# Loads in pieces between the weight tiles, squares of two chunks at a time, and low parts ahead of the next addition in a Trainium2 kernel of stacked transformer blocks

## The chip, the core and the metric

The kernel runs on one core of one Trainium2 chip. The core has five engines that each work through their own list of instructions in order: TensorE (PE, matrix products), VectorE (DVE), ScalarE (ACT), GpSimd (POOL) and SyncE (SP, which here only issues DMAs). An instruction waits on semaphores for results of other engines, and whatever stands behind it on its engine waits too. The metric is the device time of one execution in microseconds (us), lower is better. TensorE's clock is granted in two levels, 2.4 and 1.2 GHz; the profile shows it as 1.00 and 0.50.

## The reference

256 tokens (B = 1, S = 256) of width 2048 pass through two stacks of two layers each. Memory is a second sequence of 256 rows. The weights are float32 and together some 540 MB, so that each is read once.

```python
def first_block(x, mem, ...):
    memn = rms_norm(mem, norm_memory)
    for i in range(DEPTH):                       # DEPTH = 2
        h = rms_norm(x, norm_mix[i])
        if i % 2 == 0: x = x + pool_mixer(h, pool_w[ia], pool_scale[ia])
        else:          x = x + dsa_attention(h, attn_w_in[ib], attn_w_out[ib], ...)
        x = x + memory_cross_attention(rms_norm(x, norm_xattn[i]), memn, ...)
        x = x + swiglu(rms_norm(x, norm_ffn[i]), ffn_w_in[i], ffn_w_out[i])
    return rms_norm(x, norm_final)

def rms_norm(x, g):
    y = xf * lax.rsqrt(jnp.mean(xf * xf, axis=-1, keepdims=True) + EPS)
    return (y * g).astype(x.dtype)
```

The second stack follows on the result: per layer a norm, one wide input projection, four attention mixers (dilated, stick-breaking, MoBA, forgetting), and an output projection that is added back.

## The kernel before

**Layout.** The residual stream lies transposed in `XT`, 16 chunks of 128 channels by 256 tokens. Every product is computed in three parts for accuracy: an operand is split into a high part (fp32r, written by ACT, `split` L388) and a low part, the rest (written by DVE, L389). An operand chunk is thus 128x512, `[hi|lo]`; for weights ACT makes `whi` (L184) and DVE `wlo` (L194) from the raw tile `wraw`. TensorE multiplies `whi` with `[hi|lo]` and `wlo` with `hi`.

**Weights.** `Net.plan` lists all weight tiles (mostly 128x1024 float32, 512 KB) in the order of use. `_dma_to`, `_split_to` and `_lo_to` (L169 to L194) load, copy and subtract the next ones; `ahead` says how far each runs in front of the tile in use. All loads are issued by SP, in the order of the program. Raw tiles have 4 buffers.

**Start.** `mem_prep` loads the memory transposed (`memT`, 4 pieces of 512 KB) in turn with the first 4 weight tiles, then `cst`, the memory by rows (`memn`, 2 MB), the tokens by rows (`xn`, 2 MB), `band`, and then weight tiles in turn with pieces of `xT`. `kv_v` (L331, L336) computes the memory's values over 4 weight groups `xv`; beside it `mem_norm` squares `memn` on ACT (L599), and DVE computes the factor `Mn` (L587 to L416), which L430 spreads over the partitions. Four units of keys (`kv_k`) follow.

**Pool mixer.** `pool_gen` squares `xn`, computes the factor `xr`, scales `band` with it (L670, DVE), multiplies `xn` with `band` on TensorE (L677, L679) and splits the results into `X`; `pool_mix` multiplies them with the pool weights (L303 to L306) and adds into `XT` (L696).

**Residual additions.** After an output projection, `resid_pair` adds two chunks at a time from PSUM into `XT` (L506, 128x512), where the next stage's operands are split by `prep`: ACT's high parts at once, DVE's low parts later, from the list `late` that `flush` empties. `flush(1)` at the next product leaves one low part waiting. `sq_acc` squares the chunks for the next norm, the even ones on POOL (L400), the odd ones on ACT (L398), and POOL adds each to `acc` (L402, 128x256). `rowsum` (L422) sums `acc` over the partitions with two products; DVE then takes the inverse root. This happens at the stages called pool, x0 (cross attention, layer 0), x1 and b0 (second stack, layer 0); after the FFNs and the DSA attention `resid` does it with single chunks (L500, L501). With the next norm `fin` (the final norm of the first stack and the first of the second together) there are two sums, `acc` and `acc2`.

**Second stack.** Before it, at L1368 to L1381, SP loads the head gains `hg`, `fbias`, constants, `blk` and `masks`; DVE scales `hg` (L1370) and ACT copies the masks to `stickr` and `diagr`.

## Time and profile before

| what | value |
|---|---|
| time, median of 3 runs (lowest to highest) | 3086.33 us (3086.14 to 3092.42) |
| the profiled execution: time, span | 3085.38 us, 3083.5 us |
| PE busy | 3035.1 us, 98% of the span |
| DVE, ACT, POOL busy | 66%, 51%, 22% |
| mean granted clock of TensorE | 0.995 |
| read from HBM | 537.66 MB, 175 GB/s over the span |

The span is what the profiler sees from the first to the last instruction; the time of the execution is 1.9 us longer, and the median of the runs 0.95 us longer again. TensorE is busy nearly all the time, so what can be won beside fewer columns lies in two things: the few stretches in which it waits, and the few in which its clock is at 0.50, where the same column takes twice as long. Both are found by going along PE's timeline with its idle times, and along the granted clock.

### The profile page before, as it was taken

How to read it: one execution, taken by the hardware profiler on the slowest of the kernel's cores; microseconds unless marked ns; L12 is line 12 of the kernel's file. 1: busy time of each engine (PE TensorE's matmuls, PEld its weight loads, DVE VectorE, ACT ScalarE, POOL GpSimd, SP SyncE). 2: the span in 40 equal slices, each digit the busy share in tenths (PEclk: the TensorE clock that was granted, in tenths of full speed). 3: DMA queues.
4: the chain of work that ended last, by engine and by line, in shares of the span. 5: the costliest groups of instructions: out<-in, count | busy, mean ns of one | idle time of the engine just before them, and what ended most of it. 6: DMA issues, size and time to landing. Idle time of an engine off the chain costs nothing. (4 is left out here: it accounts for less than half of the span.)

```text
span 3083.5 us, 46498 instructions
## 1 busy us (share of the span) xinstructions
PE 3035.1 (98%) x17546; PEld 2646.8 (86%) x17546; DVE 2040.1 (66%) x3043; ACT 1558.1 (51%) x2470; POOL 687.5 (22%) x647
## 2 busy tenths in 40 slices
PE   7999999999999999999999999999999999999999
PEld 6888888888888888888888888888878888887888
DVE  5867555555567978755555555766786676587666
ACT  5555544544544455555344445545555555555653
POOL 0331201210223324322012102431421204341110
PEclk9999999999999999999999999999999999999999
DMA  7445566566556545466655665555655455555544
GB/s 275 156 150 198 187 192 189 190 187 190 191 175 197 181 149 177 138 194 189 192 189 188 189 191 190 176 185 176 193 148 175 130 160 184 171 185 164 160 132 156
DMA packets 158689, 550.34 MB, mean 178 GB/s; under 512 B 18464, under 2 KB 21856, under 8 KB 158176
## 3 DMA queue, kind: packets, MB, share of 16 engines
q1 hardware_dynamic: 158464, 547.36, 56.0%
q8 instruction: 138, 2.26, 0.3%
q14 instruction: 87, 0.71, 0.1%
HBM read 537.66 MB, written 2.10 MB: 175 GB/s over the span
## 5 line engine op out<-in xcount | busy, mean ns | idle before, releaser
L194 DVE TENSOR_TENSOR wlo<-wraw,whi 128x1024 fp32r<-128x1024 f32 (+1 forms) x1040 | 1286.9, 1243 | 755.6 <-ACT whi L184 389.2
L184 ACT ACTIVATE whi<-wraw 128x1024 fp32r<-128x1024 f32 (+1 forms) x1040 | 1045.6, 1025 | 630.6 <-PE mm L292 410.4
L292 PE MATMUL mm<-XOP,whi 128*128 128x512 f32 (+1 forms) x4944 | 1193.7, 393 | 11.8 <-DVE XOP L389 11.8
L292 PEld LDWEIGHTS mm<-XOP,whi 128*128 128x128 f32 (+1 forms) x4944 | 908.5, 188 | 202.3 <-DVE XOP L389 11.1
L293 PEld LDWEIGHTS mm<-XOP,wlo 128*128 128x128 f32 (+1 forms) x4944 | 636.7, 192 | 26.2 <-DVE wlo L194 1.0
L293 PE MATMUL mm<-XOP,wlo 128*128 128x256 f32 (+1 forms) x4944 | 645.6, 284 | 0.6 <-DVE wlo L194 0.5
L292 PE MATMUL mm<-hb,whi 128*128 128x512 f32 x2176 | 528.2, 392 | 1.9 <-DVE hb L386 1.9
L292 PEld LDWEIGHTS mm<-hb,whi 128*128 128x128 f32 x2176 | 397.6, 188 | 81.2 <-DVE hb L386 3.8
L796 POOL TENSOR_TENSOR t<-t,Rb 128x256 f32<-128x256 f32 x88 | 134.4, 1527 | 1078.9 <-DVE t L369 1078.9
L293 PEld LDWEIGHTS mm<-hb,wlo 128*128 128x128 f32 x2176 | 283.2, 191 | 13.1
L293 PE MATMUL mm<-hb,wlo 128*128 128x256 f32 x2176 | 287.2, 283 | 0.0
L367 ACT ACTIVATE t<-mm 128x256 f32<-128x256 f32 (+2 forms) x317 | 120.5, 380 | 183.6 <-PE mm L293 183.5
L369 DVE TENSOR_TENSOR t<-mm,t 128x256 f32<-128x256 f32 (+2 forms) x317 | 134.3, 424 | 57.4 <-ACT t L367 38.5
L798 ACT ACTIVATE t<-t 128x256 f32<-128x256 f32 x88 | 36.8, 418 | 189.0 <-POOL t L796 188.8
L385 ACT ACTIVATE hb<-t 128x256 fp32r<-128x256 f32 x120 | 50.1, 418 | 155.7 <-DVE t L805 90.5
L331 PE MATMUL mm<-whi,XOP 128*128 128x512 f32 x512 | 126.2, 399 | 0.0
L402 POOL TENSOR_TENSOR acc<-acc,t 128x256 f32<-128x256 f32 x105 | 121.0, 1153 | 21.2 <-ACT t L398 13.5
L331 PEld LDWEIGHTS mm<-whi,XOP 128*128 128x128 f32 x512 | 95.0, 188 | 21.7 <-issue 1.3
L386 DVE TENSOR_TENSOR hb<-t,hb 128x256 fp32r<-128x256 f32 x120 | 57.3, 478 | 44.5 <-ACT hb L385 44.5
L388 ACT ACTIVATE XOP<-XT,gains 128x256 fp32r<-128x256 f32 x96 | 45.3, 504 | 78.5 <-DVE XT L501 47.0
L373 POOL TENSOR_TENSOR QK<-t,Rb 128x256 f32<-128x256 f32 x40 | 38.6, 965 | 189.4 <-DVE t L369 159.3
L800 POOL TENSOR_TENSOR fs<-t,Rb 128x256 f32<-128x256 f32 x88 | 65.5, 744 | 46.5 <-ACT t L798 46.5
(270 smaller groups left out, 2407.1 us busy)
## 6 DMA issues: line engine op xcount, KB each, us to landing
wraw<-in_w_fi_dram SPq DMA_DIRECT2D x352, 512.0 KB, 4.2
wraw<-in_w_fo_dram SPq DMA_DIRECT2D x160, 512.0 KB, 3.6
wraw<-in_w_bg_dram SPq DMA_DIRECT2D x64, 512.0 KB, 4.4
wraw<-in_w_bq_dram SPq DMA_DIRECT2D x64, 512.0 KB, 4.1
wraw<-in_w_bk_dram SPq DMA_DIRECT2D x64, 512.0 KB, 5.4
wraw<-in_w_bv_dram SPq DMA_DIRECT2D x64, 512.0 KB, 3.7
wraw<-in_w_bo_dram SPq DMA_DIRECT2D x48, 512.0 KB, 3.7
wraw<-in_w_dq_dram SPq DMA_DIRECT2D x32, 512.0 KB, 4.0
```

Source lines behind the costliest of these rows:

```text
L184: self.nc.scalar.activation(hi[:, :f], t[:, :f], AF.Copy)
L194: self.nc.vector.tensor_sub(lo[:, :f], t[:, :f], hi[:, :f].bitcast(F32))
L292: lambda k, w: mm(out, w, xs[k], start=(k == 0), stop=False, skip_group_check=True),
L293: lambda k, w: mm(small, w, xs[k][:, 0:256], start=False, stop=(k == N - 1), skip_group_check=True))
L331: mm(pp[b], xs[k][:, o + b * 128:o + b * 128 + 128], w, start=(first and k == o == 0), stop=False, skip_group_check=True)
L367: nc.scalar.activation(b[0:n], ps[0:n, 256:512], AF.Copy)
L369: nc.vector.tensor_add(t[0:n], ps[0:n, 0:256], b[0:n])
L385: nc.scalar.activation(hi, src, AF.Copy)
L386: fn = lambda: nc.vector.tensor_sub(lo, src, hi.bitcast(F32))
L402: nc.gpsimd.tensor_tensor(acc, acc, q, op=OP.add)
L796: nc.gpsimd.tensor_tensor(g, self.summed(ps), self.Rb, op=OP.mult)
L800: nc.gpsimd.tensor_tensor(s2, sg, self.Rb, op=OP.mult)
```

## The change

The loads of tokens and memory are cut into pieces of 512 KB (of `memT`, the first two have 256 KB) and put on a list, `extra`; after each weight tile's DMA, one piece is taken from it. The weight tiles are split after every second chunk of the memory. `hg` is loaded at the start, and scaled after the pool mixer; the other constants of the second stack go through `extra` too, and the masks are copied eight steps later. `acc` becomes 512 wide: `prep_pair` squares two chunks in one ACT instruction, and POOL adds them in one; `rowsum` then takes four products instead of two. `resid` and `resid_pair` empty the list of low parts before the addition instead of after the next products have begun. `band` is scaled on ACT. The weights' low parts run one tile further ahead at the start of a product.

```diff
@@ -123,6 +123,7 @@
         self.hused = self.lused = 0
+        self.extra = []
         self.raw, self.hl = {}, {}
@@ -173,6 +174,8 @@
             self.nd += 1
+            if self.extra:
+                self.extra.pop(0)()
@@ -195,9 +198,9 @@
-    def ahead(self):
-        self._lo_to(self.lused + HL_BUFS - 1)
+    def ahead(self, more=0):
+        self._lo_to(self.lused + HL_BUFS - 1 + more)
         self._split_to(self.hused + HL_BUFS)
@@ -216,7 +219,7 @@
             self.hused = self.lused = i
-            self.ahead()
+            self.ahead(1)
         return (*self.hl[i], o)
@@ -226,7 +229,7 @@
         self.hused, self.lused = max(self.hused, first), max(self.lused, first)
-        self.ahead()
+        self.ahead(1)
         self._split_to(last + 1)
@@ -241,7 +244,7 @@
-    BUFS = {"t": 8, "fs2": 2, "P": 4, "PT": 3, "sq2": 3, "ny": 3, "sq": 2, "rx": 4, "rot": 1, "QK": 3, "V2": 2}
+    BUFS = {"t": 8, "fs2": 2, "P": 4, "PT": 3, "sq2": 3, "ny": 3, "sq": 2, "rx": 4, "rot": 1, "QK": 3, "V2": 2, "sp": 2}
@@ -391,14 +394,16 @@
-    def sq_acc(self, acc, src, first, fast=False):
-        nc = self.nc
-        q = acc if first else self.tmp()
+    def sq_acc(self, src, m, fast=False):
+        nc = self.nc
+        acc = self.acc[:, m % 2 * 256:m % 2 * 256 + 256]
+        q = acc if m < 2 else self.tmp()
         if fast:
...
             nc.gpsimd.tensor_tensor(q, src, src, op=OP.mult)
-        if not first:
+        if m >= 2:
             nc.gpsimd.tensor_tensor(acc, acc, q, op=OP.add)
@@ -418,8 +423,11 @@
         p = self.ps("t")
+        n = acc.shape[-1]
         for b in range(2):
-            nc.tensor.matmul(p[:, b:b + 1], acc[:, b * 128:b * 128 + 128], self.ones1, start=True, stop=True)
+            for o in range(0, n, 256):
+                nc.tensor.matmul(p[:, b:b + 1], acc[:, o + b * 128:o + b * 128 + 128], self.ones1, start=(b == o == 0),
+                                 stop=(b == 1 and o + 256 == n), skip_group_check=True)
         return p[:, 0:2]
@@ -460,7 +468,7 @@
-    def prep(self, nxt, m, fast=False):
+    def prep(self, nxt, m, sq=True):
@@ -471,7 +479,7 @@
             self.split(self.X[m], x, self.gfin2[:, m:m + 1], True)
-            self.sq_acc(self.acc, x, m == 0)
+            self.sq_acc(x, m, True)
             q = self.tmp() if m else self.acc2
@@ -479,7 +487,23 @@
             self.split(self.X[m], x, self.gain(nxt, m), True)
-        self.sq_acc(self.acc, x, m == 0, fast and m % 2 == 1 or nxt == "stat")
+        if sq:
+            self.sq_acc(x, m, nxt == "stat")
+    def prep_pair(self, nxt, m):
+        nc = self.nc
+        alone = nxt in (None, "out", "fin")
+        for c in range(2):
+            self.prep(nxt, m + c, alone)
+        if not alone:
+            q = self.acc
+            if m:
+                q = self.tmp("rot", (128, 4, 256))[:, 0:2, :].rearrange("p c t -> p (c t)") if self.second else \
+                    self.tmp("sp", (128, 512))
+            nc.scalar.activation(q, self.XT[:, m:m + 2, :].rearrange("p c t -> p (c t)"), AF.Square)
+            if m:
+                nc.gpsimd.tensor_tensor(self.acc, self.acc, q, op=OP.add)
@@ -496,16 +520,17 @@
         nc = self.nc
+        self.flush()
         x = self.XT[:, m, :]
...
     def resid_pair(self, ps, m, nxt):
+        self.flush()
         x = self.XT[:, m:m + 2, :].rearrange("p c t -> p (c t)")
         self.nc.vector.tensor_add(x, ps, x)
-        for c in range(2):
-            self.prep(nxt, m + c, True)
+        self.prep_pair(nxt, m)
@@ -595,7 +620,7 @@
             for q in range(4):
-                junk = pool.tile([128, 512], F32, name="junk", tag="junk", bufs=2)
+                junk = pool.tile([128, 512], F32, name="junk", tag="junk", bufs=1)
                 self.nc.scalar.activation(junk, src[:, b, q * 512:q * 512 + 512], AF.Square,
@@ -606,30 +631,29 @@
         self.Mb = self.b1.tile([128, 256], F32, name="Mb")
-        ts = []
-        for q in range(4):
-            t = self.XT[:, q * 4:q * 4 + 4, :]
-            nc.sync.dma_start(t, self.A["memT"][:, q * 4:q * 4 + 4, :])
-            ts.append(t)
-            self._dma_to(q + 1)
+        load = lambda t, name, *sl: self.extra.append(lambda: nc.sync.dma_start(t[:, *sl], self.A[name][:, *sl]))
+        for lo, hi in ((0, 2), (2, 4), (4, 8), (8, 12), (12, 16)):
+            nc.sync.dma_start(self.XT[:, lo:hi, :], self.A["memT"][:, lo:hi, :])
+            if lo < 12:
+                self._dma_to(self.nd + 1)
         nc.sync.dma_start(self.cst, self.A["consts"])
         self.memn = mload.tile([128, 2, D], F32, name="memn")
-        nc.sync.dma_start(self.memn, self.A["memn"])
-        if pm is not None:
-            self.xn = pm.tile([128, 2, D], F32, name="xn")
-            nc.sync.dma_start(self.xn, self.A["xn"])
-            self.band = pm.tile([128, 4, 272], F32, name="band")
-            nc.sync.dma_start(self.band, self.A["band"])
-        for q in range(4):
-            for c in range(4):
-                m = q * 4 + c
-                self.split(self.M[m], ts[q][:, c, :], self.gain(G_MEM, m), True)
-                self.flush(1)
-            self._split_to(q + 1)
-            self._lo_to(q + 1)
-            self.flush()
-            self._dma_to(q + 5)
-            nc.sync.dma_start(self.XT[:, 4 * q:4 * q + 4, :], self.A["xT"][:, 4 * q:4 * q + 4, :])
+        self.xn = pm.tile([128, 2, D], F32, name="xn")
+        self.band = pm.tile([128, 4, 272], F32, name="band")
+        for t, name in ((self.memn, "memn"), (self.xn, "xn")):
+            for b in range(2):
+                for o in (0, 1024):
+                    load(t, name, b, slice(o, o + 1024))
+        load(self.band, "band", slice(0, 4))
+        for lo in range(0, 16, 4):
+            load(self.XT, "xT", slice(lo, lo + 4))
+        load(self.hg, "hgain", slice(0, 12))
+        for m in range(16):
+            self.split(self.M[m], self.XT[:, m, :], self.gain(G_MEM, m), True)
+            self.flush(1)
+            if m % 2 and m < 8:
+                self._split_to(m // 2 + 1)
+                self._lo_to(m // 2)
         self.flush()
@@ -664,10 +688,10 @@
         r = pm.tile([128, 2], F32, name="xr")
-        yield from self.token_norm(sums, r)
+        next(self.token_norm(sums, r))
         W = self.band
         for b, (lo, hi) in enumerate(((0, 144), (144, 272))):
-            nc.vector.tensor_scalar(W[:, :, lo:hi], W[:, :, lo:hi], r[:, b:b + 1], None, op0=OP.mult)
+            nc.scalar.activation(W[:, :, lo:hi], W[:, :, lo:hi], AF.Copy, scale=r[:, b:b + 1])
         yield
@@ -685,7 +709,7 @@
     def pool_mix(self, g, nxt):
-        while self.pooled < 4 * g + 4:
+        while self.pooled < min(KC, 4 * g + 8):
             self.tick()
@@ -695,13 +719,11 @@
                                                 op0=OP.mult, op1=OP.add)
-            if g:
-                self.prep(nxt, m - 4, True)
-            if c == 1:
-                self.tick()
+            if g and c % 2:
+                self.prep_pair(nxt, m - 5)
         if g == 3:
-            for m in range(12, 16):
-                self.prep(nxt, m, True)
+            for m in (12, 14):
+                self.prep_pair(nxt, m)
@@ -1061,6 +1083,14 @@
         put(gain, y)
+    def masks_gen(self):
+        m = self.tmp("P", (128, 384))
+        self.extra.append(lambda: self.nc.sync.dma_start(m[:, 0:256], self.A["masks"]))
+        for _ in range(8):
+            yield
+        self.nc.scalar.activation(self.stickr, m[:, 0:128], AF.Copy)
+        self.nc.scalar.activation(self.diagr, m[:, 128:256], AF.Copy)
@@ -1296,11 +1326,11 @@
         self.eps = cp.tile([128, 1], F32, name="eps")
-        self.acc = cp.tile([128, 256], F32, name="acc")
+        self.acc = cp.tile([128, 512], F32, name="acc")
         self.acc2 = cp.tile([128, 256], F32, name="acc2")
...
         nc.vector.memset(self.ones1, 1.0)
-        self.fin = False
+        self.fin = self.second = False
         self.pooled = 0
@@ -1327,6 +1357,7 @@
                 with phase("poolmix") as pm:
+                    self.ph = pm
                     with phase("mload") as mload:
@@ -1345,6 +1376,8 @@
                         self.kv_k(1)
+                nc.sync.dma_start(self.fbias, A["fbias"])
+                nc.vector.tensor_scalar(self.hg[:, 0::2], self.hg[:, 0::2], 0.125, None, op0=OP.mult)
                 if "x0" in st:
@@ -1365,21 +1398,16 @@
         if "b0" in st or "b1" in st:
-            nc.sync.dma_start(self.hg, A["hgain"])
-            nc.sync.dma_start(self.fbias, A["fbias"])
-            nc.vector.tensor_scalar(self.hg[:, 0::2], self.hg[:, 0::2], 0.125, None, op0=OP.mult)
             with phase("b2") as self.ph:
                 self.cst2 = self.ph.tile([128, N_C2 * 128], F32, name="cst2")
-                nc.sync.dma_start(self.cst2, A["consts2"])
+                self.extra.append(lambda: nc.sync.dma_start(self.cst2, A["consts2"]))
                 self.stickr = self.ph.tile([128, 128], F32R, name="stickr")
...
                 self.blk = self.ph.tile([128, 128], F32, name="blk")
-                nc.sync.dma_start(self.blk, A["blocks"])
-                m = self.tmp()
-                nc.sync.dma_start(m, A["masks"])
-                nc.scalar.activation(self.stickr, m[:, 0:128], AF.Copy)
-                nc.scalar.activation(self.diagr, m[:, 128:256], AF.Copy)
+                self.extra.append(lambda: nc.sync.dma_start(self.blk, A["blocks"]))
+                self.gens.append(self.masks_gen())
                 self.fin = "b0" in st
+                self.second = True
                 if "b0" in st:
```

How the change moves instructions, at three places:

SP's list at the start of the program, before (a row is one DMA, target and source):

```order
L612 DMA XT<-in_memT_dram 128x1024
L173 DMA wraw<-in_w_xv_dram 128x1024
L612 DMA XT<-in_memT_dram 128x1024
L173 DMA wraw<-in_w_xv_dram 128x1024
L612 DMA XT<-in_memT_dram 128x1024
L173 DMA wraw<-in_w_xv_dram 128x1024
L615 DMA cst<-in_consts_dram 128x132
L617 DMA memn<-in_memn_dram 128x4096
L620 DMA xn<-in_xn_dram 128x4096
L622 DMA band<-in_band_dram 128x1088
L173 DMA wraw<-in_w_xv_dram 128x1024
L632 DMA XT<-in_xT_dram 128x1024
```

The same place after:

```order
L636 DMA XT<-in_memT_dram 128x512
L174 DMA wraw<-in_w_xv_dram 128x1024
L636 DMA XT<-in_memT_dram 128x1024
L174 DMA wraw<-in_w_xv_dram 128x1024
L636 DMA XT<-in_memT_dram 128x1024
L174 DMA wraw<-in_w_xv_dram 128x1024
L636 DMA XT<-in_memT_dram 128x1024
L639 DMA cst<-in_consts_dram 128x132
L174 DMA wraw<-in_w_xv_dram 128x1024
L634 DMA memn<-in_memn_dram 128x1024
L174 DMA wraw<-in_w_xv_dram 128x1024
L634 DMA memn<-in_memn_dram 128x1024
L174 DMA wraw<-in_w_xv_dram 128x1024
```

The 2 MB transfers of `memn` and `xn` stood ahead of the fifth `xv` tile; now the fifth tile stands ahead of them, and one quarter of `memn` behind each tile.

DVE's list at the end of the cross attention of layer 0, before: `resid_pair`'s additions (L506), the operands' low parts (L389) and the weights' low parts (L194), two steps:

```order
L194 TENSOR_TENSOR wlo<-wraw,whi 128x1024
L506 TENSOR_TENSOR XT<-mm,XT 128x512
L389 SCALAR_TENSOR_TENSOR XOP<-XT,gains,XOP 128x256 x2
L194 TENSOR_TENSOR wlo<-wraw,whi 128x1024
L506 TENSOR_TENSOR XT<-mm,XT 128x512
L389 SCALAR_TENSOR_TENSOR XOP<-XT,gains,XOP 128x256 x2
```

The same place after (L532, L392 and L197 are the same operations):

```order
L532 TENSOR_TENSOR XT<-mm,XT 128x512
L392 SCALAR_TENSOR_TENSOR XOP<-XT,gains,XOP 128x256
L197 TENSOR_TENSOR wlo<-wraw,whi 128x1024
L392 SCALAR_TENSOR_TENSOR XOP<-XT,gains,XOP 128x256
L532 TENSOR_TENSOR XT<-mm,XT 128x512
L392 SCALAR_TENSOR_TENSOR XOP<-XT,gains,XOP 128x256
L197 TENSOR_TENSOR wlo<-wraw,whi 128x1024
L392 SCALAR_TENSOR_TENSOR XOP<-XT,gains,XOP 128x256
```

In a step, the second chunk's low part stood behind the next addition; now both low parts of a pair stand ahead of it, with the weights' between them.

DVE's list before the second stack, before (L1370 scales `hg`):

```order
L500 TENSOR_TENSOR XT<-mm,XT 128x256
L501 TENSOR_TENSOR XT<-mm,XT 128x256
L1370 TENSOR_SCALAR hg<-hg 128x6
L389 SCALAR_TENSOR_TENSOR XOP<-XT,gfin_82,XOP 128x256 x2
L194 TENSOR_TENSOR wlo<-wraw,whi 128x1024 x2
```

The same place after:

```order
L525 TENSOR_TENSOR XT<-mm,XT 128x256
L526 TENSOR_TENSOR XT<-mm,XT 128x256
L392 SCALAR_TENSOR_TENSOR XOP<-XT,gfin_82,XOP 128x256
L197 TENSOR_TENSOR wlo<-wraw,whi 128x1024 x2
```

The scaling of `hg` no longer stands ahead of the last low parts, and one of these two is now done ahead of the last addition.

## Rows read from the trace of the kernel before

**Rows 1.** Stretches at half clock: bounds, length, engines' busy us, PEclk, DMA share, GB/s.

```profile
27.20:33.90 6.70, 4.63 (x11) 3.66 (x12) 2.45 (x2) 4.23 (x9) 0.00 (x0) 0.50 1.02 408
71.50:74.90 3.40, 3.40 (x17) 3.15 (x16) 1.48 (x4) 1.68 (x4) 0.00 (x0) 0.50 0.24 94
211.50:218.20 6.70, 6.33 (x25) 5.65 (x25) 6.14 (x9) 3.25 (x5) 3.20 (x4) 0.50 0.57 176
...
2034.20:2044.30 10.10, 8.81 (x33) 8.12 (x34) 5.87 (x22) 2.40 (x4) 0.00 (x0) 0.50 0.47 164
2563.30:2566.60 3.30, 3.30 (x17) 3.30 (x16) 3.03 (x5) 1.06 (x2) 0.00 (x0) 0.50 0.42 130
```

**Rows 2.** PE at the start: start, us, line, out<-in, [idle before <-releaser].

```profile
9.07 5.97 PE L331 MATMUL mm<-whi,hb 128*128 128x512 f32 x16 [9.07 <-ACT whi L184]
...
16.70 3.79 PE L331 MATMUL mm<-whi,hb 128*128 128x512 f32 x16
...
29.27 6.10 PE L331 MATMUL mm<-whi,hb 128*128 128x512 f32 x16 [6.98 <-ACT whi L184]
...
44.72 0.71 PE L430 MATMUL t<-cst,Mn 128*128 128x128 f32 x4 [2.08 <-DVE Mn L416]
```

**Rows 3.** Timeline of ACT at the start.

```profile
6.37 1.70 ACT L388 ACTIVATE hb<-XT,gains 128x256 fp32r<-128x256 f32 x4 [4.13 <-DMA XT<-in_memT_dram]
...
28.16 1.06 ACT L184 ACTIVATE whi<-wraw 128x1024 fp32r<-128x1024 f32 x1 [11.16 <-DMA wraw<-in_w_xv_dram]
```

**Rows 4.** Timeline of DVE before the memory's factor.

```profile
40.34 1.23 DVE L194 TENSOR_TENSOR wlo<-wraw,whi 128x1024 fp32r<-128x1024 f32 x1 [2.17 <-ACT whi L184]
...
44.51 0.16 DVE L416 SCALAR_TENSOR_TENSOR Mn<-rst,Mn 128x2 f32<-128x2 f32 x1
```

**Rows 5.** Timeline of PE at the pool mixer.

```profile
69.82 0.48 PE L677 MATMUL mm<-band,xn 128*128 128x144 f32 x2 [2.12 <-issue]
...
73.04 0.56 PE L303 MATMUL mm<-XOP,whi 128*128 128x256 f32 x1
...
95.56 0.39 PE L303 MATMUL mm<-XOP,whi 128*128 128x256 f32 x1 [1.29 <-DVE XT L696]
```

**Rows 6.** Timeline of DVE at the pool mixer.

```profile
69.20 1.38 DVE L670 TENSOR_SCALAR band<-band,xr 128x576 f32<-128x576 f32 x2
```

**Rows 7.** Timeline of PE before the second stack.

```profile
2035.49 1.19 PE L292 MATMUL mm<-XOP,whi 128*128 128x512 f32 x2 [4.28 <-DVE XOP L389]
```

**Rows 8.** Timeline of DVE before the second stack.

```profile
2034.79 0.17 DVE L1370 TENSOR_SCALAR hg<-hg 128x6 f32<-128x6 f32 x1 [4.73 <-DMA hg<-in_hgain_dram]
2034.87 0.87 DVE L389 SCALAR_TENSOR_TENSOR XOP<-XT,gfin,XOP 128x256 fp32r<-128x256 f32 x2
```

**Rows 9.** Timeline of ACT before the second stack.

```profile
2030.45 0.49 ACT L388 ACTIVATE XOP<-XT,gfin 128x256 fp32r<-128x256 f32 x1
```

**Rows 10.** Timeline of PE, row sums of a norm at full clock.

```profile
132.82 0.50 PE L422 MATMUL t<-ones,acc 128*128 128x1 f32 x4
```

**Rows 11.** Timeline of DVE, one step of cross attention 0's additions.

```profile
199.60 0.68 DVE L506 TENSOR_TENSOR XT<-mm,XT 128x512 f32<-128x512 f32 x1
200.21 0.47 DVE L389 SCALAR_TENSOR_TENSOR XOP<-XT,gains,XOP 128x256 fp32r<-128x256 f32 x1
200.86 0.70 DVE L389 SCALAR_TENSOR_TENSOR XOP<-XT,gains,XOP 128x256 fp32r<-128x256 f32 x1 [0.18 <-ACT XOP L388]
201.49 1.63 DVE L194 TENSOR_TENSOR wlo<-wraw,whi 128x1024 fp32r<-128x1024 f32 x1
203.04 0.68 DVE L506 TENSOR_TENSOR XT<-mm,XT 128x512 f32<-128x512 f32 x1
```

**Rows 12.** Timeline of PE after cross attention 0's additions.

```profile
211.03 0.50 PE L292 MATMUL mm<-XOP,whi 128*128 128x512 f32 x1 [2.01 <-DVE XOP L389]
```

**Rows 13.** Groups of POOL, shapes apart: xcount, busy us, mean ns, idle before.

```profile
L873 POOL TENSOR_TENSOR QK<-QK,cst 128x1024 f32<-128x1024 f32 x8 | 27.6, 3445 | 82.7 <-DMA rot<-QK 82.7
...
L873 POOL TENSOR_TENSOR QI<-QI,cosi 128x1024 f32<-128x1024 f32 x2 | 5.0, 2514 | 0.0
```

## The prediction

> **What bounds the kernel now.** I first read the busy shares: TensorE (PE) works 98% of the span, so its columns set the time, and only what it waits and what its clock loses can be won. Then I went along PE's timeline for its idle times and along the granted clock for stretches at 0.50. The losses lie in four places. At the start PE waits 6.98 us for a weight tile and later for the memory's factor [rows 2]. At the pool mixer it waits 2.12 us, and 1.29 us later on [rows 5]. After the residual additions of cross attention 0 it waits 2.01 us for low parts [rows 12]. Before the second stack it waits 4.28 us [rows 7]. After each of these the clock falls to 0.50 for 3.3 to 10.1 us [rows 1]; a stretch at half clock costs half its busy length.
>
> **Start.** Before, the fifth weight tile stood behind 4.5 MB of `memn`, `xn` and `band`, so that ACT waited 11.16 us for it and could copy it only at 28.16 [rows 3]. Where SP's list alternates 512 KB tiles and 512 KB pieces, the queue moved 408 GB/s [rows 1], which is 1.28 us for 512 KB. I carry that through the new list. The first memory piece is half as long, so ACT starts 0.64 before its 6.37 [rows 3], at 5.7; the first weight tile lands at 7.0, and with a copy of 1.06 [rows 3] PE starts at 8.1 instead of 9.07 [rows 2]. Between the first and the eighth `xv` tile stand 13.5 times 512 KB: the eighth lands at 24.3, the last piece of `memn` at 25.6, the first key tile at 26.8. PE's four value groups take 5.6 each at full clock (16.70 to its end at 22.30, where the wait of 6.98 begins [rows 2]), so 22.4, which is slower than the tiles arrive after the first two groups; for chunk splits and copies that hold up these two I add 2.2: PE ends the values at 32.7. The factor must be there as well: DVE takes the low part of the key tile ahead of it (landing 26.8, copy by about 28.9, 1.23 for the subtraction) and then the chain of small instructions, which lasts 3.1 (from 41.57, the end of the subtraction, to 44.67 [rows 4]): 33.2. So L430 comes at 33.3 instead of 44.72 [rows 2], a gain of 11.4, the halved clock of 27.2 to 33.9 included. For small waits that the order doesn't tell I take **11.0** (8 to 12). What hides the 4 MB of tokens then is the keys' work: tiles are needed every 2.8 us (half a unit of 5.6) and one tile with its piece takes 2.56.
>
> On 512 KB transfers the Trainium skill, DMA: Bandwidth & Descriptors, section Bandwidth, speaks against the change: it asks for 1 MiB or more per DMA to reach 75% of the peak. Its row for 1 MB (341 GB/s) would make a piece at least 1.54 us and the start's gain about 7, as an estimate. The trace's 408 GB/s with 512 KB transfers decides against that here.
>
> **Pool mixer.** Before, the factor's last step, two subtractions, an eviction and the two scalings of `band` (1.38 [rows 6]) stand in one row on DVE, and PE starts at 69.82 [rows 5]. On ACT the scaling takes about 1.2 (1152 columns in two instructions, where a weight copy does 1024 in 1.06 [rows 3]) and starts as soon as the factor is there, two subtractions earlier, so PE can start at once when the keys end (67.7). But two weight copies and an eviction of keys now stand behind the scaling on ACT, and DVE's second subtraction behind the first of these copies: the keys' PSUM buffer comes free 2 us later than before. I count a wait of about 1.1 in front of the third of four pairs, and the first product of the mixer at 72.7 instead of 73.04 [rows 5], with two pairs of matmuls more done (0.95 each: four steps of 0.24, half of the 0.48 that two instructions take [rows 5]). That is 2.2; of the stretch at half clock [rows 1] the part behind 73.04 is another 0.9, and the later 1.29 [rows 5] goes or stays. Sum **3.3** (1 to 5.5).
>
> **Before the second stack.** DVE's scaling of `hg` waits 4.73 for a DMA that was issued only there, and the last two low parts stand behind it [rows 8]; their high part had been written since 2030.94 [rows 9]. PE waits 4.28 [rows 7], and then its clock is at 0.50 until 2044.3, 8.8 us from 2035.5 on, of which half is lost, 4.4 [rows 1]. With `hg` there long before, the first of the two low parts is done ahead of the addition and the second right behind its high part at 2031.4; PE comes to it at 2031.2. It leaves 0.2: a gain of **8.5** (5 to 9.3, the low end where the clock still falls). The other constants now pass between weight tiles, and the masks are copied eight units later; I cost them at nothing, as 5.6 us of PE's work per unit lie over a load of 1.28, and without that cover it is rival (2).
>
> **Row sums.** Each norm sums 512 columns with four products instead of two. Two products are four instructions, 0.50 together, started 0.11 apart [rows 10]. Seven norms with four more each: 28 times 0.11, **+3.1**, all on PE.
>
> **Additions by pairs** (cross attentions 0 and 1, and the second stack's first layer, eight pairs each). DVE sets the pace there: from addition to addition 3.44 (199.60 to 203.04 [rows 11]). In the new order DVE must wait after the addition for the first high part (1.26 from the addition's start [rows 11]), then does a low part, a weight tile's low part and the second low part. Without POOL beside it, low parts take 0.40 (0.87 for two with the overlap of starts [rows 8]) and the weights' 1.14 (1.23 [rows 4] less 0.09): 1.26 + 0.40 + 1.14 + 0.40 = 3.20. At the durations that they have beside POOL in rows 11 (0.63 from start to start, then 1.55) it is 1.26 + 0.63 + 1.55 + 0.40 = 3.84. POOL's work falls from three instructions per pair to one of 128x512, which no row shows; half of the 128x1024 multiplication is 1.26 to 1.72 [rows 13]. It starts behind ACT's square, over the weights' low part. I take 3.6, nearer to the contended value, as the long DVE instruction is the one that it meets. Seven periods at +0.16 are +1.1, and behind the last addition two low parts stand instead of three, -0.4: +0.7 for each place, **+2.0** for three (-6 to +7). Whether the clock falls behind such a place is open: it costs 3.2 at one, 1.6 at another [rows 1], and is not to be worked out; 3 to either side.
>
> That low parts come ahead of the addition with single chunks, and a weight tile's low part earlier, I cost at nothing: DVE is not the bound there.
>
> **The sum.** -11.0 - 3.3 - 8.5 + 3.1 + 2.0 = -17.7. The profiled execution took 3085.4, so 3067.7; the median of the runs is 0.95 above it: 3068.6, and I say **3068**.
>
> **Rivals.** (1) *The pieces cost the queue more than large transfers.* If 512 KB took 1.71 (a quarter slower than the row), the eighth tile would land at 30.1 and the factor's chain end near 39.8: the start gives 5 instead of 11, the time is 3074. For it: no row shows small pieces from five tensors in turn at PE's first microseconds. Against it: the 408 GB/s. (2) *The stall before the second stack only changes its name*, to a weight tile behind the constants or to the masks' copies on ACT, and the clock falls all the same: the gain is 0 to 1, the time 3076. (3) *The pair additions turn out well*, at 3.2 and with no fall of the clock: -6 - 3 instead of +2, the time 3058 to 3062. (4) *POOL's 512-wide addition blocks DVE and the kernel becomes slower.* If it held DVE up for its whole length, the period would be 3.20 + 1.72 = 4.92, and 21 periods at +1.48 less 1.2 cost 30 instead of 2: 3096. It cancels the rest from a period of 4.4 on (21 times 0.96, against 19.7 of other gains). For it: beside POOL the weights' low part takes 1.63 instead of 1.23 [rows 4, 11]. Against it: that is an extension by 0.4 while POOL was busy nearly the whole period, so it doesn't stand still.
>
> The Trainium skill, SBUF — State Buffer, section SBUF: two separate sides, states the lock behind (4): a DVE instruction with two SBUF inputs and a POOL instruction that reads SBUF exclude each other, and the loser waits for the whole instruction. By that rule (4) would be the forecast where each pair's addition meets a low part at its beginning; the trace's 0.4 agrees with waits for a part of an instruction only.
>
> **How the numbers follow.** Chances: forecast 0.66; (1) 0.10; (2) 0.09; (3) 0.10; (4) 0.05. The forecast's own bounds (start 8 to 12, pool 1 to 5.5, stack 5 to 9.3, pairs and clock -6 to +7 and 3) do not all fall the same way; about half of their sum to either side gives 3060 to 3077, and with (1) and (2) and most of (3) the range 3059 to 3079 leaves out 0.2. A measurement of this kernel can tell 0.2%, 6.2 us, from no change: faster than 3080.2 holds in the forecast, (1), (2) and (3), less 0.03 for two of them together: 0.92; same 0.04, slower 0.04.
>
> **What the profile would show.** Right: the first values' matmul at about 8, no wait near 22, L430 at 33 to 34; PE's wait at the mixer's first matmuls under 0.5 with one of about 1 behind two pairs; no wait over 0.5 and no half clock before the second stack; row sums of eight instructions, 0.9 long; additions 3.4 to 3.8 apart. Wrong: waits of PE for weight tiles in the first 45 us, an ACT or DVE instruction that waits for `blk` or `masks` ahead of the second stack, or additions over 4.4 apart.

## The result, and the profile after

The changed kernel takes 3107.55 us (median of 6 runs, 3103.60 to 3109.46); the kernel before takes 3088.11 in the 6 runs that stand beside them. The ratio is 1.0059 with a 95% interval of 1.0046 to 1.0072: slower by 0.5 to 0.7%, where 3068, a range of 3059 to 3079 and a gain of 0.6% were forecast. The profiled execution took 3108.02 us, its span is 3106.2, 22.7 longer than that of the profiled execution before (the medians lie 19.4 apart).

Where the 22.7 arise follows from laying the two lists of TensorE's matmuls on each other (the row sums apart, they are the same number) and reading the difference of their start times from place to place. It is one execution against one: two executions of one kernel (e4 and e12 below) differ by up to 3 us at single places, where the clock falls in one and not in the other.

| stretch (us of the changed kernel) | change | forecast |
|---|---|---|
| start, to the mixer's first matmul at 59.2 | -10.7 | -11.0 |
| pool mixer, to 117 | -2.8 | -3.3 |
| additions of cross attention 0, 177 to 213 | +7.7 | +0.7 |
| additions of cross attention 1, 1269 to 1304 | +10.4 | +0.7 |
| in front of the second stack, 2020 to 2051 | 0.0 | -8.5 |
| attention of the second stack, both layers | +5.6 | 0 |
| additions of the second stack's first layer, 2562 to 2588 | +10.0 | +0.7 |
| the rest, with most of the row sums | +2.6 | +2 to +3 |

The first two places went as forecast. PE's timeline of the changed kernel at the start, against [rows 2] and [rows 5] (start, us, line, out<-in, [idle before <-releaser]):

```profile
7.28 6.80 PE L334 MATMUL mm<-whi,hb 128*128 128x512 f32 x16 [7.28 <-ACT whi L187]
...
21.64 3.80 PE L334 MATMUL mm<-whi,hb 128*128 128x512 f32 x16
...
34.85 0.71 PE L438 MATMUL t<-cst,Mn 128*128 128x128 f32 x4 [2.15 <-DVE Mn L421]
...
59.16 0.51 PE L701 MATMUL mm<-band,xn 128*128 128x144 f32 x2 [1.34 <-ACT band L694]
...
62.40 0.51 PE L701 MATMUL mm<-band,xn 128*128 128x144 f32 x2 [0.73 <-DVE t L372]
```

The wait of 6.98 us for the fifth weight tile is gone, and the row of L430 (now L438) stands at 34.85 instead of 44.72. The mixer waits 1.34 and 0.73. The loads in pieces moved 381 GB/s there (columns as in [rows 1]):

```profile
10.00:30.00 20.00, 19.84 (x80) 15.88 (x79) 13.87 (x22) 17.82 (x37) 0.00 (x0) 1.00 1.01 381
```

The loss sits in the additions by pairs. One step of cross attention 0 on DVE, against [rows 11]:

```profile
190.73 0.68 DVE L532 TENSOR_TENSOR XT<-mm,XT 128x512 f32<-128x512 f32 x1
191.99 0.49 DVE L392 SCALAR_TENSOR_TENSOR XOP<-XT,gains,XOP 128x256 fp32r<-128x256 f32 x1 [0.58 <-ACT XOP L391]
193.86 1.56 DVE L197 TENSOR_TENSOR wlo<-wraw,whi 128x1024 fp32r<-128x1024 f32 x1 [1.39 <-ACT whi L187]
195.34 0.47 DVE L392 SCALAR_TENSOR_TENSOR XOP<-XT,gains,XOP 128x256 fp32r<-128x256 f32 x1
195.74 0.68 DVE L532 TENSOR_TENSOR XT<-mm,XT 128x512 f32<-128x512 f32 x1
```

The same step on ACT:

```profile
191.45 0.91 ACT L391 ACTIVATE XOP<-XT,gains 128x256 fp32r<-128x256 f32 x2 [2.60 <-DVE XT L532]
192.26 0.61 ACT L504 ACTIVATE sp<-XT 128x512 f32<-128x512 f32 x1
192.78 1.05 ACT L187 ACTIVATE whi<-wraw 128x1024 fp32r<-128x1024 f32 x1
```

And POOL's addition of the pair's squares, which ends in the weights' low part:

```profile
193.02 1.32 POOL L506 TENSOR_TENSOR acc<-acc,sp 128x512 f32<-128x512 f32 x1 [3.69 <-ACT sp L504]
```

From addition to addition it is 5.01 us, against 3.44 before; the prediction had named over 4.4 as a sign of being wrong. DVE stands idle 1.39 us in front of the weights' low part (L197), for a weight copy (L187) that ACT makes behind the same pair's high parts (L391) and their square (L504): addition, high parts, square, copy, low part, low part, addition, a ring through two engines. PE waits in the ring's rhythm, and at the end for the last operands:

```profile
191.56 0.35 PE L306 MATMUL mm<-ox,whi 128*128 128x256 f32 x1 [2.02 <-DVE XT L532]
...
196.56 3.97 PE L295 MATMUL mm<-XOP,whi 128*128 128x512 f32 x11 [1.94 <-DVE XT L532]
...
202.51 0.50 PE L295 MATMUL mm<-XOP,whi 128*128 128x512 f32 x1 [1.01 <-DVE XOP L392]
205.89 0.77 PE L295 MATMUL mm<-XOP,whi 128*128 128x512 f32 x1 [2.88 <-DVE XOP L392]
```

In front of the second stack the wait of 4.28 [rows 7] has become two, though nothing waits for `hg` any more:

```profile
2042.47 0.47 PE L295 MATMUL mm<-XOP,whi 128*128 128x512 f32 x1 [2.95 <-DVE XOP L392]
2044.23 0.66 PE L295 MATMUL mm<-XOP,whi 128*128 128x512 f32 x1 [1.29 <-DVE XOP L392]
```

On DVE, ahead of the first of these two matmuls:

```profile
2040.67 1.25 DVE L197 TENSOR_TENSOR wlo<-wraw,whi 128x1024 fp32r<-128x1024 f32 x1 [1.10 <-ACT whi L187]
2041.85 0.47 DVE L392 SCALAR_TENSOR_TENSOR XOP<-XT,gfin,XOP 128x256 fp32r<-128x256 f32 x1
```

The low part that PE waits for (L392 at 2041.85) stands behind a weight tile's low part that waited 1.10 for its copy. The last four single-chunk additions ahead of this place come 4.65 us apart instead of 4.18, which loses 1.8 by 2036. The two waits are together as long as the one before (4.24 against 4.28). Behind them the clock stays at half for 3.4 us (2044.4 to 2047.8) instead of 10.1 [rows 1], and 1.8 come back.

Behind the pair additions of cross attention 1 and of the second stack the clock is at half for 10.2 us each (columns as in [rows 1]). Before, it did not fall at the first place (granted 1.00 from 1260 to 1310), and fell for 3.3 at the second [rows 1]:

```profile
1293.50:1303.70 10.20, 6.42 (x23) 5.23 (x24) 6.49 (x8) 5.94 (x9) 2.57 (x2) 0.50 0.39 112
...
2576.90:2587.10 10.20, 6.17 (x22) 4.98 (x22) 6.50 (x8) 6.27 (x10) 2.54 (x2) 0.50 0.36 111
```

### The profile page after: what moved, and what is told of

It reads as the page before. It is cut to its first block, busy times and chain, and to the rows that moved or that the text cites. A ratio compares the mean times of both kernels' runs of the same rounds, so it can differ in the third digit from the quotient of the medians.

```text
span 3106.2 us, 46523 instructions
## 1 busy us (share of the span) xinstructions
PE 3045.2 (98%) x17574; PEld 2651.6 (85%) x17574; DVE 2015.0 (65%) x3041; ACT 1572.9 (51%) x2488; POOL 606.8 (20%) x564
## 5 line engine op out<-in xcount | busy, mean ns | idle before, releaser
L197 DVE TENSOR_TENSOR wlo<-wraw,whi 128x1024 fp32r<-128x1024 f32 (+1 forms) x1040 | 1260.1, 1217 | 798.8 <-ACT whi L187 429.6
L187 ACT ACTIVATE whi<-wraw 128x1024 fp32r<-128x1024 f32 (+1 forms) x1040 | 1045.5, 1025 | 616.9 <-PE mm L295 424.9
L391 ACT ACTIVATE XOP<-XT,gains 128x256 fp32r<-128x256 f32 x96 | 45.4, 504 | 103.0 <-DVE XT L532 53.4
L389 DVE TENSOR_TENSOR hb<-t,hb 128x256 fp32r<-128x256 f32 x120 | 57.2, 477 | 44.6 <-ACT hb L388 44.6
L525 DVE TENSOR_TENSOR XT<-mm,XT 128x256 f32<-128x256 f32 x160 | 67.0, 419 | 8.2 <-PE mm L296 7.5
```

The costliest lines, as they stand in the source:

```text
L187: self.nc.scalar.activation(hi[:, :f], t[:, :f], AF.Copy)
L197: self.nc.vector.tensor_sub(lo[:, :f], t[:, :f], hi[:, :f].bitcast(F32))
L389: fn = lambda: nc.vector.tensor_sub(lo, src, hi.bitcast(F32))
L525: nc.vector.tensor_add(x, ps[:, 0:256], x)
```

## The experiments

Theory A: the weights' low parts that run one tile further ahead close the ring. Its rivals: B, the low parts ahead of the addition; C, the squares by pairs. The step between additions on DVE (median of the fourth to seventh of cross attention 0) is the measure beside the time; all times are medians, the ratios are against runs of the kernel before on the same chip.

| kernel | step, us | time, us | ratio (95% interval) |
|---|---|---|---|
| before | 3.43 | 3088 | |
| changed | 4.98 | 3107.6 | 1.0059 (1.0046 to 1.0072) |
| e1, low parts not further ahead | 4.23 | 3093.8 | 1.0031 (1.0019 to 1.0043) |
| e2, no flush ahead of the addition | 4.59 | 3090.7 | 1.0011 (1.0002 to 1.0021) |
| e3, before, low parts further ahead | 4.24 | 3104.9 | 1.0056 (1.0041 to 1.0071) |
| e4, changed without both | 2.97 | 3062.5 | 0.9922 (0.9907 to 0.9937) |
| e12, the same once more | 2.97 | 3060.8 | 0.9931 (0.9918 to 0.9943) |

**e1, the further low part undone.**

```diff
-            self.ahead(1)
+            self.ahead()
...
-        self.ahead(1)
+        self.ahead()
```

> The changed kernel with one thing undone: the weights' low parts no longer run one tile further ahead (ahead() in place of ahead(1) at both places). Theory A (DVE's low part of a weight tile now waits for a copy that ACT makes only behind the same pair's high parts and squares, so that DVE and ACT take turns): the step between additions falls from 4.98 to 3.3 to 3.7 us, the wait before the second stack under 0.5 us, the time 3066 to 3074. Rival B (low parts ahead of the addition make the chain): 3100 to 3108, step 4.7 to 5.0. Rival C (squares by pairs on ACT and the 512-wide POOL addition): also 3100 to 3108.

Measured: 3093.8, with steps of 4.23. A alone is not enough. DVE of this kernel in one step:

```profile
188.03 0.68 DVE L532 TENSOR_TENSOR XT<-mm,XT 128x512 f32<-128x512 f32 x1
189.29 0.49 DVE L392 SCALAR_TENSOR_TENSOR XOP<-XT,gains,XOP 128x256 fp32r<-128x256 f32 x1 [0.58 <-ACT XOP L391]
189.69 1.22 DVE L197 TENSOR_TENSOR wlo<-wraw,whi 128x1024 fp32r<-128x1024 f32 x1
190.82 1.51 DVE L392 SCALAR_TENSOR_TENSOR XOP<-XT,gains,XOP 128x256 fp32r<-128x256 f32 x1
192.26 0.68 DVE L532 TENSOR_TENSOR XT<-mm,XT 128x512 f32<-128x512 f32 x1
```

POOL in the same step:

```profile
190.32 1.74 POOL L506 TENSOR_TENSOR acc<-acc,sp 128x512 f32<-128x512 f32 x1 [2.49 <-ACT sp L504]
```

No instruction of DVE waits for ACT's copy any more, the weights' low part takes 1.22. But the second low part takes 1.51 instead of 0.47, and ends 0.27 after POOL's addition of the squares. None of the three had this: C named POOL's addition, but with the time unchanged.

**e2, the flush undone.**

```diff
     def resid(self, ps, m, nxt):
         nc = self.nc
-        self.flush()
...
     def resid_pair(self, ps, m, nxt):
-        self.flush()
```

> The changed kernel with only the flush ahead of the addition undone in resid and resid_pair. Theory A: the chain add, high parts, square, weight copy, weight low part stays, only one low part less in it: the step is 4.5 to 4.9 us, the time 3098 to 3106. Rival B: step 3.4 to 3.7, time 3068 to 3076. Rival C: no difference, 3105 to 3109.

Measured: 3090.7, steps of 4.59: the ring is there, as A has it, with one low part less. The time is 7 us under the range that A gave, probably since I had left out what the flush costs in front of the second stack (5 to 7, see e8).

**e3, the kernel before with the further low part alone.**

```diff
-        self._lo_to(self.lused + HL_BUFS - 1)
+        self._lo_to(self.lused + HL_BUFS - 1 + more)
...
-            self.ahead()
+            self.ahead(1)
...
-        self.ahead()
+        self.ahead(1)
```

> The kernel before with one thing added: the weights' low parts run one tile further ahead at the start of a product. Theory A: a chain of addition (0.6), high parts (0.9), square (0.4), weight copy (1.05) and weight low part (1.55) gives 4.4 to 4.6 us per step instead of 3.44: 15 to 30 us slower than before, 3103 to 3118. Rivals B and C: no change, 3085 to 3091.

Measured: 3104.9, steps of 4.24, a little under the 4.4 to 4.6 that A gave. This one edit makes the old kernel slower by 0.4 to 0.7%, and the row shows the ring:

```profile
199.91 1.41 DVE L194 TENSOR_TENSOR wlo<-wraw,whi 128x1024 fp32r<-128x1024 f32 x1 [1.09 <-ACT whi L184]
```

**e4 and e12, the changed kernel without both.**

> The changed kernel without both: neither the further low part nor the flush ahead of the addition. Theory A: about as the first of these runs, 3066 to 3076; the difference between the two is what the flush is worth (a step of 3.4 against 3.3 to 3.7, and 4 us or more before the second stack if the last low parts come late). Rival B: 3066 to 3076 too. Rival C: 3100 to 3108.

> The fourth run's kernel once more, with more rounds, for its ratio: 3059 to 3066, 0.6% to 0.9% faster than before, steps of 2.98 us.

Measured: 3062.5 and 3060.8, 0.6 to 0.9% faster than before, below what A gave. DVE's step:

```profile
189.84 0.68 DVE L530 TENSOR_TENSOR XT<-mm,XT 128x512 f32<-128x512 f32 x1
190.44 1.31 DVE L392 SCALAR_TENSOR_TENSOR XOP<-XT,gains,XOP 128x256 fp32r<-128x256 f32 x2
191.68 1.22 DVE L197 TENSOR_TENSOR wlo<-wraw,whi 128x1024 fp32r<-128x1024 f32 x1
192.81 0.68 DVE L530 TENSOR_TENSOR XT<-mm,XT 128x512 f32<-128x512 f32 x1
```

POOL beside the first two of these rows:

```profile
189.15 1.92 POOL L506 TENSOR_TENSOR acc<-acc,sp 128x512 f32<-128x512 f32 x1 [1.05 <-ACT sp L504]
```

A step takes 2.97, and no idle time of DVE is listed in it. So both edits cost, each alone 28 to 31 us on top of e4, together 40 to 42 by the ratios and 45 by the medians. C falls: with the squares by pairs, the step is shorter than before.

**e6, e7 and e11: is it POOL's addition that holds DVE?** Theory D: POOL's 512-wide addition and a low part on DVE exclude each other. e6 is e1 without that addition, e11 the changed kernel without it.

```diff
-            if m:
-                nc.gpsimd.tensor_tensor(self.acc, self.acc, q, op=OP.add)
```

> The first run (changed kernel without the further low part, with the flush) with POOL's 512-wide addition of the squares left out, so that the norms behind the pair additions get a sum of two chunks only. Theory D (POOL's addition and DVE's second low part exclude each other, so DVE waits for POOL's whole instruction): that low part falls from 1.51 to about 0.42 us, the step from 4.23 to 3.0 to 3.3, the time to 3066 to 3078. Rival E (the low part is long because ACT's high part or the square comes late): it stays 1.4 to 1.6 and the step 4.1 to 4.3, the time 3090 to 3096.

> The changed kernel itself with POOL's 512-wide addition of the squares left out (the norms behind the pair additions get a sum of two chunks only). The chain through ACT is untouched: the weights' low part falls from 1.54 to 1.22 us and the step from 4.98 to 4.6 to 4.7, time 3095 to 3103. If POOL made the chain too, as it did in the first run: step 3.0 to 3.6, time 3066 to 3078.

e6: 3072.1 (ratio 0.9958, 0.9945 to 0.9971), steps of 3.19, and the second low part at 0.48:

```profile
189.42 0.48 DVE L392 SCALAR_TENSOR_TENSOR XOP<-XT,gains,XOP 128x256 fp32r<-128x256 f32 x1
189.81 0.68 DVE L530 TENSOR_TENSOR XT<-mm,XT 128x512 f32<-128x512 f32 x1
```

e11: 3103.7 (1.0065, 1.0052 to 1.0079), a microsecond above its range, steps of 4.67 with the wait for the copy unchanged:

```profile
188.19 1.22 DVE L197 TENSOR_TENSOR wlo<-wraw,whi 128x1024 fp32r<-128x1024 f32 x1 [1.38 <-ACT whi L187]
```

So D holds, and there are two mechanisms: without the further low part, POOL's addition makes the step; with it, the ring does, and POOL adds 0.3 to the weights' low part. In the changed kernel POOL's addition thus makes only 0.31 of a step of 4.98, and in time its removal is not told from chance (1.0065 against 1.0059).

This also tells why e4 is quick though POOL adds there too. Behind the weights' low part DVE has the addition from PSUM (L530), which takes 0.68 beside POOL's addition and 0.68 without one (e6). Only the low parts behind it still wait: two of them take 1.31, where two without POOL take 0.87 [rows 8]. And the third step of e4's cross attention 0 takes 4.78 instead of 3.43: its low parts take 2.01 and the weights' 2.33 beside two additions of POOL.

In e7 the square moves behind the weight copy, which takes 0.5 out of the ring and moves POOL's addition onto the second low part:

```diff
+        self.squares_due()
         alone = nxt in (None, "out", "fin")
...
-            nc.scalar.activation(q, self.XT[:, m:m + 2, :].rearrange("p c t -> p (c t)"), AF.Square)
-            if m:
-                nc.gpsimd.tensor_tensor(self.acc, self.acc, q, op=OP.add)
+            def square():
+                nc.scalar.activation(q, self.XT[:, m:m + 2, :].rearrange("p c t -> p (c t)"), AF.Square)
+                if m:
+                    nc.gpsimd.tensor_tensor(self.acc, self.acc, q, op=OP.add)
+            self.sqs.append(square)
```

> The changed kernel with ACT's square of a pair put behind the weight copy instead of ahead of it. The chain alone (addition, high parts, weight copy, weight low part, second low part, without the 0.5 of the square): steps of 4.4 to 4.6 instead of 4.98, time 3094 to 3101. With theory D as well, POOL's addition now falls on the second low part: that takes 1.5 or more and the step stays at 4.9 to 5.6, time 3104 to 3120.

Measured: 3110.7 (1.0076, 1.0051 to 1.0102), steps of 5.15. The wait for the copy falls to 0.86, and the gain is lost to the exclusion, as DVE's rows show:

```profile
193.41 1.23 DVE L198 TENSOR_TENSOR wlo<-wraw,whi 128x1024 fp32r<-128x1024 f32 x1 [0.86 <-ACT whi L188]
194.56 1.50 DVE L393 SCALAR_TENSOR_TENSOR XOP<-XT,gains,XOP 128x256 fp32r<-128x256 f32 x1
```

and POOL's beside them:

```profile
194.04 1.74 POOL L509 TENSOR_TENSOR acc<-acc,sp 128x512 f32<-128x512 f32 x1 [3.44 <-ACT sp L507]
```

**e8, the flush in resid alone, on e4.**

```diff
     def resid(self, ps, m, nxt):
         nc = self.nc
+        self.flush()
```

> The fourth run with the flush put back in resid alone (single chunks), not in resid_pair. If the flush there makes the wait before the second stack (the last low parts stand behind two weight low parts, whose copies stand behind ACT's squares): PE waits 2.9 and 1.3 us again and its clock falls, 6 to 10 us more than that run: 3068 to 3073. If not: 3060 to 3065, with the wait of 0.55.

Measured: 3068.8 (0.9941, 0.9920 to 0.9963), 5 to 7 more than e4 (6.4 by the medians, 5.6 by the profiled executions), with intervals that overlap. What is clear is the place: between 2000 and 2050 the traces of e8 and e4 run apart by 6.9, of which 1.8 arise in the last four single-chunk steps (4.65 instead of 4.18). The two waits of the changed kernel are back to the hundredth:

```profile
2020.98 0.47 PE L295 MATMUL mm<-XOP,whi 128*128 128x512 f32 x1 [2.95 <-DVE XOP L392]
2022.74 0.80 PE L295 MATMUL mm<-XOP,whi 128*128 128x512 f32 x1 [1.29 <-DVE XOP L392]
```

So it is the flush that put a new wait where that for `hg` was.

**e10, `hg` loaded late again, on e4.** The load and the scaling stand in front of the second stack.

> The fourth run with the head gains loaded and scaled in front of the second stack again, the other constants still between weight tiles. If that load made the wait of 4.28 us there: the wait is back at 3 to 5 us and the clock falls behind it, 5 to 9 us more than the fourth run: 3067 to 3072. If another step removed the wait: no change, 3060 to 3065.

Measured: 3068.7 (0.9954, 0.9938 to 0.9969), 6 to 8 more than e4 and e12, and 6.4 by the traces of e10 and e4 between 2010 and 2060; the wait is 5.09, and DVE's row is that of [rows 8] again:

```profile
2020.71 0.17 DVE L1398 TENSOR_SCALAR hg<-hg 128x6 f32<-128x6 f32 x1 [4.12 <-DMA hg<-in_hgain_dram]
```

**e9, the start undone, on e4.** The memory and the tokens come in transfers of 2 MB ahead of the fifth weight tile.

> The fourth run with the start undone: the memory and the tokens in transfers of 2 MB ahead of the fifth weight tile, as before. If the pieces won what the traces say (10 us and more up to the first product of keys' row 40, the wait of 7 us for a weight tile gone): 3071 to 3076, that is 9 to 13 more than the fourth run, and the wait of 6 to 8 us near 22 is back. If the gain belongs to something else in the change: 3060 to 3066.

Measured: 3072.0 (0.9960, 0.9947 to 0.9974), 9.6 more than e4 and 11.2 more than e12; at 200 us the trace of e9 lies 7.8 behind that of e4 and 8.8 behind that of e12, and the wait is back:

```profile
28.36 5.79 PE L334 MATMUL mm<-whi,hb 128*128 128x512 f32 x16 [7.19 <-ACT whi L187]
```

**e5, the squares by pairs undone, on e4.** Single squares, one half on POOL, sums of 256 columns, two products for a row sum.

> The fourth run (changed kernel without the further low part and without the flush) with the squares by pairs undone too: single squares, one half of them on POOL, 256-wide sums, two products for a row sum. If squares by pairs relieve DVE at the additions (POOL's three instructions per pair become one): steps of 3.4 instead of 2.98 us and waits of 2 us behind each of the three places come back, less 3.1 us of row sums: 3064 to 3073. If they only cost row sums: 3058 to 3061.

Measured: 3068.7 (0.9943, 0.9921 to 0.9965). Steps are 3.43 again, and behind cross attention 0 PE waits 2.01 and 0.37 as before, against 1.51 in e4. The medians say 6 to 8 us for the pairs, the two profiled executions 1 (3064.2 and 3063.2), and the intervals of e5 and e4 overlap: that the pairs relieve DVE is shown, what they are worth in sum beside 3.1 us of row sums is not settled.

## Why the prediction was wrong

**Start: right.** PE began at 7.28 where I had 8.1, L430 came at 34.85 where I had 33.3; 10.7 was gained for 11.0, and e9 gives 8 to 11. PE ended the values at 32.7, as forecast. Rival (1) fell: the queue moved 381 GB/s with the pieces, not the 306 of a quarter less than 408, and behind the first tile PE waited for no weight tile in the changed kernel's start. The Trainium skill (DMA: Bandwidth & Descriptors, Bandwidth) asks for a MiB or more per DMA to reach 75% of the peak; the trace outweighs that here, for 512 KB transfers that stand in a queue behind each other.

**Pool mixer: right in size** (-2.8 for -3.3), not in its waits, so the size is in part luck. The first wait is 1.34, where I had PE start at once and named under 0.5 as the sign: the keys end at 57.8, the factor is there only at 58.3, and the first half of ACT's scaling stands in between. In front of a later pair it is 0.73, where I had 1.1.

**Row sums: right.** Behind cross attention 0 the sums take eight instructions (PE's timeline of the changed kernel):

```profile
211.71 0.95 PE L429 MATMUL t<-ones,acc 128*128 128x1 f32 x8
```

That is 0.95 where four took 0.50 [rows 10], 0.45 each time.

**Second stack: wrong by 8.5.** The mechanism of the old wait was right: without the flush (e4, e12) the place gains 7.0 against the kernel before, by the traces, and with `hg` late again (e10) 6.4 of that go. The step that failed is "the first of the two low parts is done ahead of the addition": I read that as a gain, from the order of DVE alone. It stands there behind two weight low parts, and the copy for the second of them stands on ACT behind that chunk's own high part and two squares. That is the ring once more, with single chunks. Rival (2) had the right form (the stall changes its name) and the right size (a gain of 0 to 1, measured 0.0), and the wrong name.

**Additions by pairs: wrong by 26 in three places.** The step that failed is the term "a weight tile's low part earlier, I cost at nothing: DVE is not the bound there". By itself it takes the old kernel's step from 3.43 to 4.24 and costs 17 to 19 us (e3). The sum for DVE without POOL, 3.20, was right (3.19 in e6); what the account left out is the wait for ACT's copy. DVE's list reads the same with and without the edit when the tiles' numbers are left out; what differs is which tile the low part belongs to. With the tiles' numbers, the orders tell them apart. Before, an addition (of mm_1891), and the weights' low part behind it on DVE:

```
L506 TENSOR_TENSOR XT_75<-mm_1891,XT_75 128x512
L389 SCALAR_TENSOR_TENSOR XOP_76<-XT_75,gains_79,XOP_76 128x256 x2
L194 TENSOR_TENSOR wlo_1936<-wraw_1765,whi_1896 128x1024
```

The copy that it needs, on ACT, and the high parts of that addition's pair behind it:

```
L184 ACTIVATE whi_1896<-wraw_1765 128x1024
L388 ACTIVATE XOP_76<-XT_75,gains_79 128x256 x2
L398 ACTIVATE t_1930<-XT_75 128x256
```

After, the addition (of mm_1870) and the low part:

```
L532 TENSOR_TENSOR XT_75<-mm_1870,XT_75 128x512
L392 SCALAR_TENSOR_TENSOR XOP_76<-XT_75,gains_79,XOP_76 128x256
L197 TENSOR_TENSOR wlo_1913<-wraw_1785,whi_1911 128x1024
```

and its copy on ACT, behind that pair's high parts and square:

```
L391 ACTIVATE XOP_76<-XT_75,gains_79 128x256 x2
L504 ACTIVATE sp_1906<-XT_75 128x512
L187 ACTIVATE whi_1911<-wraw_1785 128x1024
```

Before, the copy was made ahead of the pair's high parts, a step earlier; now behind them. One place in the list, and a cover of a whole step was gone. I had looked for what is queued behind the moved instruction on DVE, and not for what its input is queued behind on ACT.

The second mechanism is rival (4), to which I gave 0.05 on the ground that the weights' low part takes only 0.4 longer beside POOL. That reading was wrong: a wait for the rest of an instruction that already runs shows as a short stretch when that one is nearly done. In the changed kernel the weights' low part starts 0.48 before POOL's addition ends, and takes 0.34 longer than without it (1.56 against 1.22 in e11). In e1, POOL's addition begins beside the weights' low part and takes 1.74 (1.32 when it starts alone, in the changed kernel); the low part behind it takes 1.51, and without POOL (e6) 0.48. That agrees with the rule that the prediction cited from the Trainium skill (SBUF — State Buffer, SBUF: two separate sides): the loser waits for the whole instruction. Rival (4) deserved a larger chance: with a 512-wide addition ready while a weight's low part runs, the low part behind that one waited for all of it in each step of e1. Its price in e1 is 1.04 per step, so the step is 4.23 and not 4.9 as rival (4) had it. In time it is 22 us (e1 against e6), about what e4 gains; with the wait in front of the second stack (e8) it makes e1 slower than the kernel before. In the changed kernel itself it is the lesser part, 0.31 of each step (e11).

**The sum.** The span came out 40 above the sum (+22.7 for -17.7). Of the 22.8 forecast for the start, the mixer and the second stack, 13.5 came, which is 9 of the 40; 26 arose in the pair additions and 5.6 in the second stack's attention. Of that last part, waits of PE for `P` at L583 (1.60 and 1.37 us in the changed kernel) and the half clock behind them, I know only that such waits lie anywhere between 0.4 and 2.3 us in the other kernels too, whichever edits they have; what sets them is open.

## What to carry to other kernels

When an instruction is moved ahead, follow its inputs to the engine that makes them and ask what they are queued behind there, with the numbers of the tiles: an order that reads the same can belong to another tile. A prefetch in two passes (a copy on one engine, a remainder on another) needs a step of distance between them, and the work that waits for a result must not stand between the two. Where two engines exclude each other, put the long instruction of the one beside work of the other that it doesn't hold up: in e4 POOL's addition runs beside DVE's addition from PSUM. The changed loads, squares and constants without the two edits gained 0.7 to 0.8% (e4, e12).

## What the runs showed of the hardware

An instruction's length in the profile can hold its wait for the other engine: DVE's 128x256 low part shows as 1.51 us beside POOL's addition and as 0.48 without, POOL's 128x512 addition as 1.32 or 1.74, and that part of the wait is not in the idle time listed in front of them. A step whose parts are all busy can thus be a chain of waits. And an edit that shortens a chain can lengthen the step, where it moves POOL's work onto another instruction of DVE (e7: 0.5 less in the ring, 0.17 more in the step).
